# Two transformer blocks on one core: PSUM bank order at the start of two feed-forward layers, and a new placement of output and memory tiles between eight attention heads

## The chip, the cores and the metric

One Trainium2 chip, one core of it. The metric is the device time of one launch in microseconds (us), lower is better. The kernel is written in Python with a tile scheduler: the program states the operations, and the scheduler decides the order on each engine (TensorE = PE, VectorE = DVE, ScalarE = ACT, GpSimd = POOL, SyncE = SP, which here only issues loads).

## The reference

Two blocks over 512 tokens of width 1024, all in fp32. The change touches the two feed-forward layers and the second block's attention:

```python
# first block, after its two attention branches
h = rms_norm(x, pre_ffn_norm)
f = (silu(h @ w_ffn_gate) * (h @ w_ffn_up)) @ w_ffn_down        # 1024 -> 2816 -> 1024
x = x + rms_norm(f, post_ffn_norm)
# second block
fox_o = fox_attention(fq, fk, fv, log_f)                        # 8 heads of 64
z = einsum(q, k) / 8                                            # stick-breaking, 8 heads of 64
log_keep = where(strict, log_sigmoid(-z), 0)
after = reverse_cumsum(log_keep) - log_keep
a = where(strict, exp(log_sigmoid(z) + after), 0)
sb_o = einsum(a, v)
x = x + concat(rmsnorm(fox_o), rmsnorm(sb_o)) @ w_out
x = x + memory_cross_attention(rmsnorm(x), rmsnorm(mem), w_mq, w_mkv, w_mo)   # 256 memory rows
u = conv3(rmsnorm(x) @ w_up)                                    # width 2 * 2816
x = x + (silu(u_gate) * u_val) @ w_down
return rmsnorm(x)
```

## The kernel before, in words

**Matmuls.** Activations lie as 128 x 512 tiles (features on partitions, tokens along the row). Every fp32 operand is split into a high and a low part; `mm3` multiplies a pair by a pair with three matmuls: high by high (L208 in the profile), low by high (L209) and high by low (L210). `wload` loads 128 x 1024 of a weight on SP's queue into one of three buffers (`wr0` to `wr2`); ACT casts the high part (`wh`, L136) and DVE subtracts for the low part (`wl`, L140). A load into a buffer has to wait for the casts out of it. `lin` makes one output tile: a load or two, then 3 matmuls for each 128 rows of the weight, into one PSUM bank.

**Banks.** There are eight PSUM banks of 128 x 512. `share(mm=..., at=..., op=..., st=...)` deals them to four rings by use: `MM()` for linear layers, `AT()` for attention scores, `OP()` for attention outputs, `ST()` for sums of squares. Each call takes the next bank of its ring, so a ring with one bank makes its users wait for one another.

**Norms.** `Stat.done` sums squares with a ones-matmul (L376), takes the inverse root on POOL (`rtok`, L333), turns it with four transposes (L384) into a bank, and copies that bank on ACT to `R` (L390).

**Feed-forward layers.** `first_halves` makes the first six linear tiles in two halves of 256 tokens, so that the first half can begin before the norm of the second is known; it uses banks 0 to 5 for the sums, and 6 and 7 for the sums of squares and `R`. Then come six more `lin`s (L1040 and L1519, from ring 0 to 5 still) and eight tiles of the down projection, each over the six hidden tiles made so far. After that both layers deal all eight banks to `mm`.

**Stick-breaking heads** (L1357 to L1383). The loop runs over nine steps; step `hd` makes the scores and log-keep tiles of head `hd` (`sb_keep`: score matmuls into ring `at`, banks 3 to 6; ACT abs, exp, ln; DVE `e` L1233, `lkh` L1235, `lkl` L1236) and the values of the head before it (`sb_values`: score matmuls again, L1245, L1246, and sums of log-keep L1250, L1251; ACT exp to `aw`, then `ah`; DVE `al`; then `pv2_step`, L1209 and L1210, which add the four query blocks into bank 7, the only bank of ring `op`). At the end of a head `pv2_out` copies half of bank 7 on ACT (`tmp`, L1215) and adds it to the other half on DVE (`so`, L1217). The next head's first L1209 needs bank 7, and so `so`. A short wait of this sort is hidden if other matmuls stand ahead of it.

**Fillers.** For that, `between(fill[hd])` puts tiles of other work behind step `hd`: `y0` to `y7` are output tiles over the forgetting heads (12 matmuls 128x512 each), `k0` to `k7` keys of the memory (24 matmuls 128x256 and one load of 512 KB), `v0` and `v1` values of the memory (48 matmuls 128x512 and four loads of 512 KB). The ninth entry comes after the loop. The scheduler may shift them against the heads, but keeps each engine's work near its place in the program.

**After the loop.** The sums of squares of `so` (L376), tiles of `fill[8]`, four output tiles over `so` (12 matmuls 128x512, `boh`), then the `R` of this norm, then four more output tiles in halves of 256 tokens (`last_halves`) of which the second, in order, takes bank 5 that held the transposes for `R`; then the weights of the cross attention's query (`w_mq`), which ACT casts in the same order in which it copies `R`.

Of the kernel before, what the change touches and what calls it, by code (L numbers as in the profile page):

```python
# [58 lines left out]
def two_blocks(ctx: ExitStack, tc: tile.TileContext, d, dbg=None):  # L59
# [16 lines left out]
    def A(name, dt=F32, cols=T):  # L76
        if cols > 256 or len(spare_half) < 3:
            i = spare.popleft()
            low[0] = min(low[0], len(spare))
            ap = ar.tile([P, T], dt, tag="slot%d" % i, name=name)[:, :cols]  # L80
            owner[id(ap)] = (spare, i, ap, name)
        else:
            i = spare_half.popleft()
            ap = ar.tile([P, 256], dt, tag="half%d" % i, name=name)[:, :cols]
            owner[id(ap)] = (spare_half, i, ap, name)
        return ap

    def free(*xs):
        for x in xs:
            if isinstance(x, (tuple, list)):  # L90
                free(*x)
            else:
                home, i = owner.pop(id(x))[:2]
                home.append(i)
# [13 lines left out]
    def share(**kw):  # L108

        for name, which in kw.items():  # L110
            rings[name] = deque(which)
# [48 lines left out]
    def order(later, earlier):  # L160
        tc.add_manual_dep(later, earlier.name,
                          mybir.DependencyInfo(mybir.DependencyClass.NoSync, mybir.DependencyReason.DATA),
                          reason="table of functions")
# [35 lines left out]
    def wpart(wt, k):  # L199

        step, ws = wt
        hi, lo = ws[k // step][k % step // 4]
        s = slice(k % step % 4 * P, (k % step % 4 + 1) * P)
        return hi[:, s], lo[:, s]

    def mm3(ps, a, b, first, last):
        (ah, al), (bh, bl) = a, b
        r = PE.matmul(ps, lhsT=ah, rhs=bh, start=first, stop=False)  # L208
        PE.matmul(ps, lhsT=ah, rhs=bl, start=False, stop=False)  # L209
        PE.matmul(ps, lhsT=al, rhs=bh, start=False, stop=last)  # L210
        return r.ins
# [35 lines left out]
    def tok_step(ps, h, t, w, first, last):  # L247
        q = slice(t * P, (t + 1) * P)
        return mm3(ps, (h[0][:, q], h[1][:, q]), w, first, last)
# [85 lines left out]
    class Stat:  # L335


        def __init__(self, n, cols=T, esq=None, eadd=None, late=False):
            self.n, self.cols, self.acc, self.late, self.wait = n, cols, {}, late, {}
            self.esq, self.eadd = esq or S, eadd or V  # L340
            self.R, self.r = None, RTOK()
            self.sums, self.turns = {}, {}
# [24 lines left out]
        def done(self, c=None, direct=False):  # L367
# [18 lines left out]
            if direct:  # L386
                return pb[:, :w]
            if self.R is None:
                self.R = A("R")
            S.copy(self.R[:, c], pb[:, :w])  # L390
            return self.R, self.r

# [67 lines left out]
    def evac(ps, name, Rt, scale=None, cols=T):  # L460
        o = A(name)
        if scale is None:
            V.tensor_tensor(o[:, :cols], ps[:, :cols], Rt[:, :cols], ALU.mult)
        else:
            V.scalar_tensor_tensor(o[:, :cols], ps[:, :cols], scale, Rt[:, :cols], ALU.mult, ALU.mult)
        return o
# [29 lines left out]
    def first_halves(at, ns, wts, hs, st, out, before=None, tok=None, tok_out=None):  # L496

        for i, c in enumerate(HALVES):  # L500
            st.done(c)
            ts = range(2 * i, 2 * i + 2) if tok else ()
            tps = [MM() for t in ts]
            pss = [MM() for n in ns]
            last = len(hs) - 1

            def after(r, step):
                for m, earlier in marks:
                    if m == step:
                        order(r, earlier)  # L510

            def tok_k(k, step):
                for t, ps in zip(ts, tps):
                    after(tok_step(ps, hs[k], t, tok[k], k == 0, k == last), step)

            def lin_k(k, j, step):
                hh, hl = hs[k]
                after(mm3(pss[j][:, :256], wpart(wts[j], k), (hh[:, c], hl[:, c]), k == 0, k == last), step)

            if i == 0:  # L520
                marks = [(at[0], st.sums[0]), (at[1], st.turns[0])]
                if before:
                    marks.append((at[2], before.turns[256]))
                for k in range(len(hs)):
                    tok_k(k, k)
                    for j in range(len(ns)):
                        lin_k(k, j, k)
            else:

                marks = [(at[3], st.sums[256]), (at[4], st.turns[256])]  # L530
                for k in range(len(hs)):
                    tok_k(k, k - len(hs))
                for j in range(len(ns)):
                    for k in range(len(hs)):
                        lin_k(k, j, j if k == 0 else None)
            for t, ps in zip(ts, tps):
                tok_out(t, ps)
            for j, n in enumerate(ns):
                out(n, pss[j][:, :256], c)
        free([wt[1] for wt in wts])  # L540
        free(tok or [])
# [80 lines left out]
    st = Stat(DM, esq=S, eadd=V)  # L622
# [16 lines left out]
    free(xs)  # L639
    R, rt = st.done()  # L640
    p0 = evac(pss[0], "p0", R)
# [60 lines left out]
    for t, ps in enumerate(lin_tok(d["w1K"], 0, hs)):  # L702
        x = A("kdx")
# [283 lines left out]
    st = Stat(DM)  # L987
# [28 lines left out]
        V.tensor_tensor(firsts[n][:, c], ps, sth.R[:, c], ALU.mult)  # L1016

    first_halves((6, 7, 3, 2, 4), range(6), ws, hs, sth, first_out, st)
    R = sth.R
    fs = [None] * KD  # L1020
    hid = []
# [5 lines left out]
    st = Stat(DM)  # L1027
# [323 lines left out]
    Rf, _ = stf.done()  # L1351
    close = closing(so, sts, "sb_g")

    fill = [x.split() for x in ('y0 y1 k0 y2|y3 y4|k1 k2|y5 y6 y7 k3|k4 k5||v0 v1||k6 k7').split("|")]

    def between(what, after=None):
        for w in what:  # L1357
# [11 lines left out]
    for hd in range(9):  # L1369
        lks = []  # L1370
        if last:
            op = OP()
# [115 lines left out]

    firsts = {}
    first_halves((2, 3, None, 0, 3), range(6), ws, hs, sth, first_out)  # L1490
    R = sth.R
    hid = []
    st = Stat(DM, late=True)
# [203 lines left out]
```

## Time and profile before

| | |
|---|---|
| median of 3 runs | 1735.14 us (1735.02 to 1739.23) |
| profiled execution | 1737.63 us, its span 1735.8 us, 1.8 us around it |
| PE busy | 1703.2 us (98%), weight loads 1487.2 us (86%) |
| DVE, ACT, POOL busy | 69%, 51%, 5% |
| DMA | 174.30 MB, mean 100 GB/s |
| TensorE's granted clock | full speed in every fortieth of the span |

The span is the time from the first to the last instruction of the profiled execution. In the timeline each row has a start, a duration, engine, line, operation, output and inputs, shape, and in brackets the idle time ahead of it with the instruction that ended it. Matmuls are pipelined: a row's duration is longer than what it adds, so what one matmul costs is read from start to start of two neighbours.

### The profile page before, as it was taken

What the parts mean: (1) busy time and instruction counts of PE and PEld (TensorE: products, weight loads), DVE (VectorE), ACT (ScalarE), POOL (GpSimd) and SP (SyncE); (2) the same over time, 40 slices, a digit from 0 to 9 for tenths busy, and PEclk for the clock granted to TensorE, in tenths of its full rate; (3) what the DMA queues carried; (4) which work ended last, traced back from release to release, by engine and by line L of the source; (5) the groups of instructions that cost most, each with busy time, mean ns of one, the idle gap of its engine ahead of it and who ended that gap; (6) DMA issues with size and microseconds to landing.
All of it is one profiled execution on the core that took longest, in us unless ns stands there. A gap on an engine that the chain in (4) does not pass through costs nothing.

```text
span 1735.8 us, 25856 instructions
## 1 busy us (share of the span) xinstructions
PE 1703.2 (98%) x9706; PEld 1487.2 (86%) x9706; DVE 1197.7 (69%) x2390; ACT 885.5 (51%) x1821; POOL 92.5 (5%) x109
## 2 busy tenths in 40 slices
PE   9999999999999999999999999998999999999998
PEld 7888888888888889989988888887898988988987
DVE  7547764677667757757777666787866598964863
ACT  6534454565444444424445666786525454552653
POOL 1000001000004000000022000000200200000000
PEclk9999999999999999999999999999999999999999
DMA  6212252223640332433324345333314123232321
GB/s 226 85 49 73 66 171 89 75 77 96 200 158 1 107 100 72 125 97 98 123 85 122 96 111 128 103 110 115 117 50 134 50 70 100 92 118 83 103 92 50
DMA packets 63950, 174.30 MB, mean 100 GB/s; under 512 B 8080, under 2 KB 13392, under 8 KB 63824
## 3 DMA queue, kind: packets, MB, share of 16 engines
q1 hardware_dynamic: 63408, 172.44, 32.4%
q8 instruction: 76, 1.25, 0.3%
q14 instruction: 50, 0.41, 0.1%
q10 hardware_dynamic: 288, 0.14, 0.0%
q0 software_dynamic: 128, 0.07, 0.0%
HBM read 153.74 MB, written 4.19 MB: 91 GB/s over the span
## 4 chain that ended last, share of the span: by engine, by line
PE 84%; DVE 7%; ACT 3%; DMA 3%; issue 2%; POOL 1%; POOLq 0%; DVEq 0%; ACTq 0%
PE bank L208 26%; PE bank L210 26%; PE bank L209 26%; DVE wl L140 1%; DMA wr<-w_o_mla 1%; PE bank L1250 1%; DVE hl L142 1%; ACT wh L136 1%; PE bank L828 1%; DVE f L976 1%; DMA wr<-w_mq 1%; DVE sq L362 1%; DMA wr<-w1K 0%; PE bank L1209 0%; PE bank L1210 0%
## 5 line engine op out<-in xcount | busy, mean ns | idle before, releaser
L136 ACT CAST wh<-wr 128x512 fp32r<-128x512 f32 (+2 forms) x534 | 310.7, 605 | 364.4 <-PE bank L209 122.1
L140 DVE TENSOR_TENSOR wl<-wr,wh 128x512 fp32r<-128x512 f32 (+1 forms) x534 | 349.8, 673 | 167.1 <-ACT wh L136 145.8
L208 PE MATMUL bank<-hh,wh 128*128 128x512 f32 (+1 forms) x868 | 306.2, 355 | 1.9 <-DVE z L1016 1.7
L210 PE MATMUL bank<-hh,wl 128*128 128x512 f32 (+1 forms) x868 | 305.9, 354 | 0.8 <-DVE wl L140 0.8
L209 PE MATMUL bank<-hl,wh 128*128 128x512 f32 (+1 forms) x868 | 305.4, 353 | 0.1
L209 PE MATMUL bank<-prl,wh 128*128 128x256 f32 (+1 forms) x760 | 253.5, 334 | 0.0
L210 PE MATMUL bank<-prh,wl 128*128 128x256 f32 (+1 forms) x760 | 253.3, 334 | 0.0
L208 PE MATMUL bank<-prh,wh 128*128 128x256 f32 (+1 forms) x760 | 251.3, 334 | 0.6 <-ACT prh L136 0.6
L210 PEld LDWEIGHTS bank<-hh,wl 128*128 128x128 f32 x868 | 164.7, 190 | 23.2 <-DVE wl L140 2.1
L208 PEld LDWEIGHTS bank<-hh,wh 128*128 128x128 f32 x868 | 164.6, 190 | 23.0 <-ACT hh L138 1.9
L209 PEld LDWEIGHTS bank<-hl,wh 128*128 128x128 f32 x868 | 164.8, 190 | 20.9 <-DVE hl L142 0.6
L208 PEld LDWEIGHTS bank<-prh,wh 128*128 128x128 f32 x760 | 144.3, 190 | 15.0 <-ACT prh L136 1.0
L210 PEld LDWEIGHTS bank<-prh,wl 128*128 128x128 f32 x760 | 144.4, 190 | 14.3 <-DVE wl L140 0.4
L209 PEld LDWEIGHTS bank<-prl,wh 128*128 128x128 f32 x760 | 144.4, 190 | 13.7
L209 PE MATMUL bank<-nl,wh 128*128 128x512 f32 (+1 forms) x440 | 148.4, 337 | 0.0
L208 PE MATMUL bank<-nh,wh 128*128 128x512 f32 (+1 forms) x440 | 148.3, 337 | 0.0
L210 PE MATMUL bank<-nh,wl 128*128 128x512 f32 (+1 forms) x440 | 147.9, 337 | 0.0
L208 PEld LDWEIGHTS bank<-nh,wh 128*128 128x128 f32 x440 | 83.5, 190 | 9.0
L209 PEld LDWEIGHTS bank<-nl,wh 128*128 128x128 f32 x440 | 83.5, 190 | 8.8
L210 PEld LDWEIGHTS bank<-nh,wl 128*128 128x128 f32 x440 | 83.5, 190 | 8.8
L333 POOL TENSOR_TENSOR rtok<-sm,minus_half 128x2 f32<-128x2 f32 (+1 forms) x20 | 17.5, 877 | 1203.0 <-DVE sm L332 1203.0
L136 ACT CAST wh<-s 128x512 fp32r<-128x512 f32 x72 | 43.8, 619 | 69.2 <-DVE s L297 40.4
(400 smaller groups left out, 3357.7 us busy)
## 6 DMA issues: line engine op xcount, KB each, us to landing
wr<-w_up SPq DMA_DIRECT2D x38, 512.0 KB, 3.6
wr<-w_fgu SPq DMA_DIRECT2D x32, 512.0 KB, 4.0
wr<-w1T SPq DMA_DIRECT2D x16, 512.0 KB, 3.5
wr<-w_gate SPq DMA_DIRECT2D x16, 512.0 KB, 4.0
wr<-w_fd SPq DMA_DIRECT2D x16, 512.0 KB, 4.0
wr<-w2T SPq DMA_DIRECT2D x16, 512.0 KB, 3.8
wr<-w_dn SPq DMA_DIRECT2D x16, 512.0 KB, 3.5
wr<-w1K SPq DMA_DIRECT2D x12, 512.0 KB, 4.3
```

What stands on the lines that cost most here:

```text
L136: r = S.copy(hi, src) if eh is S else V.tensor_copy(hi, src)
L140: q = el.tensor_tensor(lo, src, f(hi), ALU.subtract)
L142: q = V.scalar_tensor_tensor(lo, src, scale, f(hi), ALU.mult, ALU.subtract)
L208: r = PE.matmul(ps, lhsT=ah, rhs=bh, start=first, stop=False)
L209: PE.matmul(ps, lhsT=ah, rhs=bl, start=False, stop=False)
L210: PE.matmul(ps, lhsT=al, rhs=bh, start=False, stop=last)
L333: G.tensor_tensor(y, v, minus_half[:, :y.shape[1]], ALU.pow)
L362: i = self.eadd.tensor_tensor(acc, acc, q[:, :w], ALU.add)
L828: PE.transpose(tp[:, i * P:(i + 1) * P], ps_tiles[i][:, b * P:(b + 1) * P], C("ident"))
L976: r = V.scalar_tensor_tensor(fs[k][:, c], fs[k][:, c], vcol(gain, k), st.R[:, c], ALU.mult, ALU.mult)
L1250: PE.matmul(z[:, (b2 - b) * P:w], lhsT=lt, rhs=part[:, :T - b2 * P], start=False, stop=False)
```

## The change

Three edits. Behind `first_halves` of each feed-forward layer the ring of banks is dealt anew: all eight to `mm`, in the order 6, 7, 0 to 5 (before: the six banks 0 to 5 go on). And the list of fillers is another.

```diff
@@ -1016,6 +1016,7 @@
     first_halves((6, 7, 3, 2, 4), range(6), ws, hs, sth, first_out, st)
+    share(mm=(6, 7, 0, 1, 2, 3, 4, 5), at=(), op=(), st=())
     R = sth.R
@@ -1351,7 +1352,7 @@
-    fill = [x.split() for x in ('y0 y1 k0 y2|y3 y4|k1 k2|y5 y6 y7 k3|k4 k5||v0 v1||k6 k7').split("|")]
+    fill = [x.split() for x in ('k0 y0 y1|y2 y3 y4|k1 y5 y6|y7 k2 k3|v0|k4 k5|v1|k6|k7').split("|")]
@@ -1488,6 +1489,7 @@
     first_halves((2, 3, None, 0, 3), range(6), ws, hs, sth, first_out)
+    share(mm=(6, 7, 0, 1, 2, 3, 4, 5), at=(), op=(), st=())
     R = sth.R
```

By step of the loop (0 to 7, then after it) the fillers stand so:

| step | 0 | 1 | 2 | 3 | 4 | 5 | 6 | 7 | after |
|---|---|---|---|---|---|---|---|---|---|
| before | y0 y1 k0 y2 | y3 y4 | k1 k2 | y5 y6 y7 k3 | k4 k5 | none | v0 v1 | none | k6 k7 |
| changed | k0 y0 y1 | y2 y3 y4 | k1 y5 y6 | y7 k2 k3 | v0 | k4 k5 | v1 | k6 | k7 |

Lines behind L1018 are one higher in the changed kernel, behind L1490 two.

What this does to the order is shown at three places. In these rows the number behind a name tells buffers apart, and a bracket names the engine that the row waits for.

**PE at the change from head 6 to head 7**, before: the last matmuls of head 6 into bank 7, then the first of head 7.

```order
L1250 MATMUL bank6_72<-lkl_12242,incl_r_172 128x128
L1251 MATMUL bank6_72<-nstrict_r_178,ident_r_176 128x128
L1209 MATMUL bank7_73<-ah_12252,v2_10506 128x128 [waits Activation_49]
L1210 MATMUL bank7_73<-al_12253,v2_10506 128x128 [waits DVE_49]
L1209 MATMUL bank7_73<-ah_12274,v2_10488 128x512 [waits DVE_49]
L1210 MATMUL bank7_73<-al_12275,v2_10488 128x512
L1209 MATMUL bank7_73<-ah_12291,v2_10494 128x384 [waits Activation_49]
```

And in the changed kernel (L1210 is its first line of a head's output):

```order
L208 MATMUL bank2_68<-boh_12049,wh_12464 128x512
L209 MATMUL bank2_68<-bol_12050,wh_12464 128x512
L210 MATMUL bank2_68<-boh_12049,wl_12465 128x512
L210 MATMUL bank0_66<-boh_11180,wl_12425 128x512 [waits DVE_49]
L208 MATMUL bank0_66<-boh_11617,wh_12424 128x512
L209 MATMUL bank0_66<-bol_11618,wh_12424 128x512
L210 MATMUL bank0_66<-boh_11617,wl_12425 128x512
L208 MATMUL bank0_66<-boh_12049,wh_12424 128x512
L209 MATMUL bank0_66<-bol_12050,wh_12424 128x512
L210 MATMUL bank0_66<-boh_12049,wl_12425 128x512
L1210 MATMUL bank7_73<-ah_12313,v2_10488 128x512 [waits Activation_49]
L1211 MATMUL bank7_73<-al_12314,v2_10488 128x512 [waits DVE_49]
```

Before, nothing stands between the last matmul of head 6 into bank 7 and the first of head 7. In the changed order 18 matmuls 128x512 of output tiles over `so` (10 are shown) stand directly ahead of head 7's first, and ahead of these head 7's score matmuls; these 18 stood further back before.

**PE behind the loop**, where the transposes for `R` stand. Before, they lie among output tiles of the full 512 tokens, and the matmul that needs bank 5 again (`boh_11180` with `wh_12509`) comes 24 rows later:

```order
L208 MATMUL bank1_67<-boh_11617,wh_12444 128x512
L209 MATMUL bank1_67<-bol_11618,wh_12444 128x512
L384 MATMUL bank5_71<-con_160,rtok8_117 128x128 [waits Pool_49]
L384 MATMUL bank5_71<-con_160,rtok8_117 128x128 x3
L210 MATMUL bank1_67<-boh_11617,wl_12445 128x512
L208 MATMUL bank1_67<-boh_11957,wh_12444 128x512
```

In the changed kernel it comes 5 rows later:

```order
L208 MATMUL bank4_70<-boh_12049,wh_12504 128x256
L209 MATMUL bank4_70<-bol_12050,wh_12504 128x256
L384 MATMUL bank5_71<-con_160,rtok8_117 128x128 [waits Pool_49]
L384 MATMUL bank5_71<-con_160,rtok8_117 128x128 x3
L210 MATMUL bank4_70<-boh_12049,wl_12505 128x256
L208 MATMUL bank4_70<-boh_12370,wh_12504 128x256
L209 MATMUL bank4_70<-bol_12371,wh_12504 128x256
L210 MATMUL bank4_70<-boh_12370,wl_12505 128x256
L208 MATMUL bank5_71<-boh_11180,wh_12509 128x256 [waits Activation_49]
```

The transposes moved behind matmuls that followed them before, and the wait for `R` moved close behind them. From the L376 matmuls to that wait there are 18 matmuls 128x512, 12 of 128x256 and the transposes in the changed order. On ACT the copy `R` stands behind eight casts of four `w_mq` loads before and, in the changed kernel, behind six casts of three; of the first `w_mq` load both casts stand between `tmp` of head 7 and the squares of `so` there.

**PE in the second feed-forward layer's down projection**, where the sixth hidden tile (`prh_14666`) is first used. Before:

```order
L209 MATMUL bank4_70<-prl_14583,wh_14783 128x512
L210 MATMUL bank4_70<-prh_14582,wl_14784 128x512
L209 MATMUL bank5_71<-prl_14583,wh_14811 128x512
L210 MATMUL bank5_71<-prh_14582,wl_14812 128x512
L208 MATMUL bank0_66<-prh_14386,wh_14861 128x512 [waits Activation_49]
L209 MATMUL bank0_66<-prl_14387,wh_14861 128x512
L208 MATMUL bank2_68<-prh_14666,wh_14701 128x512 [waits Activation_49]
```

In the changed kernel:

```order
L210 MATMUL bank2_68<-prh_14498,wl_14944 128x512
L208 MATMUL bank2_68<-prh_14582,wh_14947 128x512
L209 MATMUL bank2_68<-prl_14583,wh_14947 128x512
L210 MATMUL bank2_68<-prh_14582,wl_14948 128x512
L208 MATMUL bank0_66<-prh_14386,wh_14861 128x512 [waits Activation_49]
L209 MATMUL bank0_66<-prl_14387,wh_14861 128x512
L208 MATMUL bank4_70<-prh_14666,wh_14701 128x512 [waits Activation_49]
```

With two more banks one more output tile (bank 2, `wh_14943`) can begin before the sixth hidden tile is there: 15 of its matmuls 128x512 now stand ahead of the waiting row. In the first feed-forward layer the order of PE is the same as before but for the numbers of the banks.

## Rows read from the trace of the kernel before

**Rows 1.** The page: its span, the busy time of each engine, and the granted clock of TensorE in 40 equal slices (9 is 90% or more of full speed).

```profile
span 1735.8 us, 25856 instructions
PE 1703.2 (98%) x9706; PEld 1487.2 (86%) x9706; DVE 1197.7 (69%) x2390; ACT 885.5 (51%) x1821; POOL 92.5 (5%) x109
PEclk9999999999999999999999999999999999999999
```

**Rows 2.** The waits of PE within the loop over the stick-breaking heads (1086 to 1213.4 us): what waited for what, us in total, times, longest.

```profile
PE bank L1209 <- DVE so L1217: 4.6, 3, 2.4
PE bank L1245 <- ACT aw L171: 1.4, 3, 0.6
PE bank L1245 <- DVE e L1233: 1.1, 1, 1.1
PE bank L210 <- DVE wl L140: 0.8, 2, 0.4
```

**Rows 3.** The timeline of PE, six of the matmuls that waited there: start, duration, and in brackets the wait.

```profile
1113.14 0.50 PE L1245 MATMUL bank<-dbl,stk 128*128 128x512 f32 x1 [0.63 <-ACT aw L171]
...
1159.52 0.50 PE L1209 MATMUL bank<-ah,v 128*128 128x512 f32 x1 [1.44 <-DVE so L1217]
...
1163.69 0.33 PE L1245 MATMUL bank<-dbl,stk 128*128 128x128 f32 x1 [0.62 <-ACT aw L171]
...
1172.90 0.51 PE L1209 MATMUL bank<-ah,v 128*128 128x512 f32 x1 [0.68 <-DVE so L1217]
...
1203.13 0.50 PE L1245 MATMUL bank<-dbl,stk 128*128 128x512 f32 x1 [1.06 <-DVE e L1233]
...
1209.91 0.50 PE L1209 MATMUL bank<-ah,v 128*128 128x512 f32 x1 [2.45 <-DVE so L1217]
```

**Rows 4.** Busy time by stretch, each from the first L1209 of one head to that of the next (heads 2 to 3, 3 to 4, 4 to 5, 5 to 6, 6 to 7): length, then busy us and instructions of PE, PEld, DVE, ACT, POOL, the granted clock, the DMA engines' share and GB/s.

```profile
1131.04:1148.43 17.39, 16.99 (x118) 15.67 (x117) 15.75 (x35) 14.04 (x33) 0.00 (x0) 1.00 0.67 182
1148.43:1159.52 11.09, 9.65 (x71) 9.17 (x69) 8.48 (x21) 8.01 (x20) 0.00 (x0) 1.00 0.16 49
1159.52:1172.90 13.38, 12.02 (x72) 10.49 (x73) 11.60 (x26) 12.79 (x32) 0.00 (x0) 1.00 0.13 39
1172.90:1198.24 25.34, 25.16 (x119) 20.84 (x119) 18.13 (x35) 17.65 (x37) 0.00 (x0) 1.00 0.44 136
1198.24:1209.91 11.67, 8.16 (x59) 7.51 (x57) 8.16 (x18) 9.10 (x25) 0.00 (x0) 1.00 0.21 69
```

**Rows 5.** The timeline of DVE, ACT and PE at the change from head 6 to head 7: the last log-keep tile of head 7, head 6's last matmul into bank 7, and the two steps of its output.

```profile
1205.24 0.29 DVE L1236 SCALAR_TENSOR_TENSOR lkl<-e,lkh 128x128 fp32r<-128x128 f32 x1
...
1207.19 0.28 PE L1210 MATMUL bank<-al,v 128*128 128x128 f32 x1
...
1208.56 0.58 ACT L1215 COPY tmp<-bank 64x512 f32<-64x512 f32 x1
...
1209.18 0.68 DVE L1217 TENSOR_TENSOR so<-bank,tmp 64x512 f32<-64x512 f32 x1
```

**Rows 6.** The timeline of PE: neighbours of 128x512 and of 128x256, for the step from start to start.

```profile
1220.71 0.40 PE L208 MATMUL bank<-boh,wh 128*128 128x512 f32 x1
1220.94 0.39 PE L209 MATMUL bank<-bol,wh 128*128 128x512 f32 x1
...
1229.48 0.28 PE L209 MATMUL bank<-bol,wh 128*128 128x256 f32 x1
1229.60 0.28 PE L210 MATMUL bank<-boh,wl 128*128 128x256 f32 x1
```

**Rows 7.** The timeline of PE behind the loop: the sums of squares, the transposes, and the matmul that takes bank 5 again.

```profile
1219.12 0.95 PE L376 MATMUL bank<-con,sq 128*128 128x2 f32 x8
...
1226.40 0.60 PE L384 MATMUL bank<-con,rtok 128*128 128x128 f32 x4
...
1232.12 0.39 PE L208 MATMUL bank<-boh,wh 128*128 128x256 f32 x1 [1.17 <-ACT R L390]
```

**Rows 8.** The timeline of ACT behind the loop: the squares of the last `so`, three of the four pairs of `w_mq` casts, and the copy of `R`.

```profile
1217.25 0.63 ACT L349 ACTIVATE sq<-so 128x512 f32<-128x512 f32 x1 [0.99 <-DVE so L1217]
...
1224.62 1.15 ACT L136 CAST wh<-wr 128x512 fp32r<-128x512 f32 x2 [1.50 <-DMA wr<-w_mq]
...
1227.64 1.14 ACT L136 CAST wh<-wr 128x512 fp32r<-128x512 f32 x2 [1.88 <-DMA wr<-w_mq]
...
1230.32 1.14 ACT L136 CAST wh<-wr 128x512 fp32r<-128x512 f32 x2 [0.20 <-DMA wr<-w_mq]
1231.48 0.59 ACT L390 COPY R<-bank 128x512 f32<-128x512 f32 x1
```

**Rows 9.** DMA issues of `w_mq`: count, KB each, and the median us from issue to landing; of those issued from 1215 to 1216 us, of those from 1220 to 1222.6 us, and of all.

```profile
wr<-w_mq SPq DMA_DIRECT2D x1, 512.0 KB, 3.7
...
wr<-w_mq SPq DMA_DIRECT2D x3, 512.0 KB, 6.2
...
wr<-w_mq SPq DMA_DIRECT2D x8, 512.0 KB, 4.0
```

**Rows 10.** The timeline of PE: the longest wait in the first feed-forward layer, and the one in the second.

```profile
560.30 0.36 PE L208 MATMUL bank<-hh,wh 128*128 128x256 f32 x1 [1.72 <-DVE z L1016]
...
1448.18 0.50 PE L208 MATMUL bank<-prh,wh 128*128 128x512 f32 x1 [0.62 <-ACT prh L136]
```

## The prediction on record

> **What bounds the kernel now.** I read the page first. PE is busy 1703.2 of 1735.8 us, the next engine, DVE, 69%, and TensorE has its higher clock level, 2.4 GHz, in all 40 slices (granted share 0.9 or more) [rows 1]. So the kernel is a chain of matmuls, and since the change adds and removes no matmul, no cast and no load, it can win only what PE waits: 1735.8 - 1703.2 = 32.6 us over the whole span. The next view is PE's waits within the loop over the stick-breaking heads. They come to 4.6 + 1.4 + 1.1 + 0.8 = 7.9 us, and over half of it is a head's first output matmul waiting for bank 7, that is for the output `so` of the head before [rows 2]. The timeline says where: 1.44, 0.62 and 0.68 us from 1159 to 1173, 1.06 and 2.45 us from 1203 to 1210 [rows 3]. The busy time by stretch says why. From head 5 to head 6 both memory-value tiles stand, and PE is idle 25.34 - 25.16 = 0.18 us; from head 2 to 3 it is idle 0.40 us. From 3 to 4 it is 11.09 - 9.65 = 1.44, from 4 to 5 1.36, from 6 to 7 11.67 - 8.16 = 3.51 us [rows 4]. The last three are the starved stretches: 6.3 us together. The chain that PE waits for there is fixed: head 6's last matmul into bank 7 starts at 1207.19, `tmp` follows at 1208.56, `so` ends at 1209.18 + 0.68 = 1209.86 [rows 5], and head 7 starts at 1209.91 [rows 3]. To hide it, some 2.5 us of other matmuls have to stand in between.
>
> **The change, part by part.** PE's unit prices are steps from start to start: 128x512 takes 1220.94 - 1220.71 = 0.23 us, 128x256 0.12 us [rows 6].
>
> *Fillers, what they hide.* From head 6 to 7 nothing stood between; the changed order puts 18 matmuls 128x512 directly ahead of head 7's first, 18 x 0.23 = 4.1 us, and head 7's score matmuls too, more than the 2.5 us wanted. The memory-value tiles (48 x 0.23 = 11.0 us each) no longer stand together in a stretch that idled 0.18 us anyway: one goes to the stretch of 1.44 us. The key tiles (24 x 0.12 = 2.9 us each) stand in steps 5 and 7, one of which was empty. All three starved stretches so get more than their wait. I take the whole 6.3 us as removed: **-6.3**. The bounds are 0 (the waits only move) and -7.9 (all of the loop's waits go).
>
> *Fillers, what is late next.* Every moved tile brings its loads on SP, its casts on ACT and its subtractions on DVE. The stretch from head 4 to 5 already has ACT busy 12.79 of 13.38 us [rows 4]: there ACT, not PE, sets the pace, and two more casts of `wh` at 0.57 each (1.15 for two) [rows 8] fall into heads that had none. I take 0.8 us for that. On DVE `lkl` of head 7 (0.29) now stands behind `so` (0.68) and so behind `tmp` (0.58) [rows 5]; PE's sums of log-keep wait for it: half of 1.55, 0.7 us. And the 18 matmuls ahead of head 7 need three `w_out` tiles cast in time, where before they came later: 0.8 us, the cast and subtraction of one tile less what its two buffers of lead give. Together **+2.3**, bounds 0 and 4.9 (twice the largest wait that stands there now, 2.45 [rows 3]). The loads themselves cost nothing: the stretch with eight value loads moved 136 GB/s and the one with `y` tiles 182 GB/s, both with PE idle under 0.5 us [rows 4], and the changed list spreads them. Without that cover a load costs what one of `w_mq` takes, about 4 us [rows 9].
>
> *Behind the loop.* What is used to hide head 7 is missing later. The sums of squares end at 1219.12 + 0.95 = 1220.07; the matmul that takes bank 5 again could have started at 1232.12 - 1.17 = 1230.95 [rows 7]. So before 10.9 us of matmuls stand from the sums to this wait. Now there are 18 x 0.23 + 12 x 0.12 + the transposes, 0.45 = 6.0 us. The copy of `R` ends at 1231.48 + 0.59 = 1232.07, 12.0 us after the sums, and it is late because it stands on ACT behind `w_mq` casts that wait for loads (1.50, 1.88, 0.20 us) [rows 8]. If it stays at 12.0, PE waits 6.0 instead of 1.2 us; if it only needs its transposes, it ends some 6.1 us after the sums and PE waits 0.1. So the term is between +4.9 and -1.1. In the changed order three pairs of casts stand ahead of it, not four, which takes off 1.3 us (a pair and its wait: 1.14 + 0.20) and leaves 10.7. Of the waits for loads, 1.50 + 1.88 + 0.20 = 3.6 us, I take off half, 1.8, since the order lets the first of these loads out before the sums and not behind them. That makes 8.9 us, about the middle of 12.0 and 6.1: a wait of 2.9 us in place of 1.2, **+1.7**.
>
> *Second feed-forward layer.* PE waits 0.62 us there for the sixth hidden tile [rows 10]. The changed order puts 15 matmuls of another output tile, 15 x 0.23 = 3.4 us, ahead of it: **-0.6**. If the two banks were not free, the wait would be as before, 0.
>
> *First feed-forward layer.* Its order is the same, and its one long wait, 1.72 us [rows 10], lies within `first_halves`, ahead of the new line. **0**; the two banks go to tiles that wait for nothing now.
>
> The sum: -6.3 + 2.3 + 1.7 - 0.6 = -2.9 us. The profiled execution took 1737.63 us (span 1735.8 and 1.8 around it), 2.5 us above the median of the runs, 1735.14. The terms are differences, so I set them against both: 1734.7 for an execution like the profiled one, **1732.2 us** as the median.
>
> **The rivals.** I call a difference under 0.3% (5.2 us: 1729.9 to 1740.3) no change, as it is about what a measurement of this kernel can tell.
>
> *Loads come sooner, and the gain stays.* The last `w_mq` loads before took 6.2 us each, three at once, while one alone took 3.7 [rows 9]. If the spread list leaves them alone, they land 2.5 us sooner: `R` ends some 6.9 us after the sums, PE waits 0.9 us (-0.3 against before instead of +1.7), and the 0.8 us for `w_out` go: -6.3 + 1.5 - 0.3 - 0.6 = -5.7, 1729.4 us. For it: fewer loads stand right behind the loop. Against it: the three go out within 2.4 us in either order. The Trainium skill, "DMA: Bandwidth & Descriptors", section "Anatomy of one DMA", fits a DMA (on GpSimd's path, these are on SP's) with about 2.0 us plus its bytes over 436 GB/s, which for 512 KB gives an estimate of 3.2 us whatever else is in flight. By that rule this rival is the forecast; the rows, 6.2 us for three at once, disagree.
>
> *The waits only move.* ACT's 96% in the stretch from head 4 to 5 becomes the pace of more stretches, with as much idle as before, and the tail loses what the order adds: -6.3 + 4.9 + 1.7 - 0.6 = -0.3, 1734.8 us. For it: ACT is busy 12.79 us where PE is 12.02 [rows 4]. Against it: where the value tiles stand, PE has 25.16 us for ACT's 17.65, and the changed list uses that surplus twice.
>
> *Slower: `R` behind the casts.* The squares of `so`, on ACT, now stand behind the first `w_mq` pair; if this load takes 6.2 us and not 3.7, the sums come 2.5 us late with little left to hide it, and `R` still comes 12.0 us after them, behind three more pairs. That is +2.5 + 4.9. With 4.9 of new waits in the loop it would be -6.3 + 4.9 + 2.5 + 4.9 - 0.6 = +5.4, 1740.5 us. `R` decides: the change loses there from the point where it ends more than 6.0 + 1.2 = 7.2 us after the sums, and the whole is slower than before once the loop and layers keep less than that loss. For it: the order of ACT's queue is fixed, and its row shows a wait for `w_mq` ahead of every pair [rows 8]. Against it: it takes the late end of three terms at once.
>
> **How the numbers follow.** The forecast, 0.52: its own range is 1729.5 to 1735. Loads sooner, 0.26: 1727.5 to 1731. Waits only move, 0.15: 1733 to 1737. Slower, 0.07: 1737 to 1742. Faster by over 0.3% takes most of the second case, 0.22 of 0.26, and the low end of the first, 0.08: 0.30. Slower is the last case, 0.07, and no change the rest, 0.63. The range from 1727.5 to 1737.0 leaves out the last case and the tails of the others, under 2 in 10.
>
> **What would show it.** In the changed kernel's profile: no wait of head 7's first output matmul (L1210 there) for `so`, and starved stretches with under 1 us idle; `lkl` or `wl` as the new releasers within the loop, 1 to 4 us in all; behind the loop, the wait of the matmul into bank 5 for ACT's `R` at 2 to 4 us, where it was 1.17, with `w_mq` loads as what ACT waits for ahead of it; no wait for `prh` in the second layer's down projection; nothing new in the first. I am wrong if `so` still ends waits of over 2 us, if the wait for `R` is under 1 or over 5 us, if the head stretches idle as much as before, or if waits arise in a feed-forward layer that had none.

## The result, and the profile after

The changed kernel takes **1726.23 us** (median of 6 runs, 1724.92 to 1726.83), the kernel before 1736.05 us (6 runs): a ratio of 0.9941 with a 95% interval of 0.9930 to 0.9951. It is faster by 9.8 us, outside the forecast range and more than three times the forecast gain of 2.9 us. The profiled execution took 1726.83 us. Its page, to be held against [rows 1]:

```profile
span 1725.1 us, 25847 instructions
PE 1700.7 (99%) x9706; PEld 1485.8 (86%) x9706; DVE 1197.4 (69%) x2390; ACT 886.9 (51%) x1821; POOL 92.0 (5%) x109
PEclk9999999999999999999999999999999999999999
```

PE's idle time fell from 32.6 to 1725.1 - 1700.7 = 24.4 us, 8.2 us less. Its busy time fell too, by 2.5 us, with the same 9706 matmuls. Of these, 1.4 us lie in the places named below, where something of a wait is counted as busy; the rest lies ahead of the heads, 0.7 us of it in the first 28 us.

**Where the time came from.** Both traces have the same number of matmuls in each stage, so the n-th matmul of one (counted by start, from 0) can be laid beside the n-th of the other wherever the order agrees again:

| matmul, place | start before | start after | difference | won in this stretch |
|---|---|---|---|---|
| 5830, ahead of the heads | 1070.74 | 1069.72 | -1.02 | 1.0 |
| 6805, output tiles behind the heads | 1240.84 | 1232.84 | -8.00 | 7.0 |
| 6949, cross attention's first halves | 1260.46 | 1250.94 | -9.52 | 1.5 |
| 8100, second feed-forward layer | 1438.34 | 1428.77 | -9.57 | 0.05 |
| 8254, behind its first down projection | 1470.99 | 1460.26 | -10.73 | 1.2 |
| 9705, the last | 1729.10 | 1718.36 | -10.74 | 0.0 |

Of the first 1.0 us, 0.5 is there by matmul 100 (28 us) and 0.9 by matmul 500 (115 us), ahead of everything that the change touches. The executions of the other runs start matmul 5830 between 2.1 us earlier and 1.5 us later than that of the kernel before, so this is a difference between two executions. The other 9.7 us lie in three places: the heads, the cross attention's first halves and the second feed-forward layer.

**The heads.** PE's waits in the loop (1083 to 1213 us) answer to [rows 2]:

```profile
PE bank L208 <- ACT wh L136: 0.7, 1, 0.7
PE bank L1246 <- ACT aw L171: 0.5, 1, 0.5
PE bank L1211 <- DVE al L140: 0.2, 1, 0.2
```

No wait for `so` is left; 4.6 us in three waits stood there. By stretch from head to head (2 to 3, and so on to 6 to 7; columns as in [rows 4]):

```profile
1125.31:1144.30 18.99, 18.77 (x127) 17.29 (x127) 15.91 (x35) 16.01 (x38) 0.00 (x0) 1.00 0.62 168
1144.30:1163.86 19.56, 19.56 (x117) 17.49 (x117) 13.65 (x27) 13.55 (x31) 0.00 (x0) 1.00 0.42 133
1163.86:1180.13 16.27, 15.74 (x99) 13.72 (x98) 14.21 (x32) 14.49 (x38) 0.00 (x0) 1.00 0.22 66
1180.13:1196.12 15.99, 15.99 (x97) 14.35 (x96) 11.65 (x24) 11.90 (x25) 0.00 (x0) 1.00 0.33 99
1196.12:1208.84 12.72, 12.17 (x68) 9.90 (x67) 9.81 (x23) 9.94 (x26) 0.00 (x0) 1.00 0.24 82
```

Length less PE's busy time gives 0.22, 0, 0.53, 0 and 0.55 us, 1.3 together; in [rows 4] it was 0.40, 1.44, 1.36, 0.18 and 3.51, 6.9. The lengths themselves are now even, 13 to 20 us instead of 11 to 25. At the change from head 6 to 7 PE, ACT and DVE show why:

```profile
1201.52 0.33 PE L1211 MATMUL bank<-al,v 128*128 128x128 f32 x1
...
1201.88 0.58 ACT L1216 COPY tmp<-bank 64x512 f32<-64x512 f32 x1 [0.98 <-PE bank L1211]
...
1202.50 0.68 DVE L1218 TENSOR_TENSOR so<-bank,tmp 64x512 f32<-64x512 f32 x1
...
1208.62 0.39 PE L210 MATMUL bank<-boh,wl 128*128 128x512 f32 x1
1208.84 0.39 PE L1210 MATMUL bank<-ah,v 128*128 128x512 f32 x1
```

`so` is there at 1203.18, and head 7's first matmul comes 5.7 us later, right behind the `boh` matmuls and without a wait. The chain is covered, and it is shorter as well: `tmp` and `so` take the same 0.58 and 0.68 us as in [rows 5], but `tmp` starts 0.36 us behind the start of head 6's last matmul instead of 1.37. Before, `aw` and `ah` of head 7 stood ahead of `tmp` on ACT, the last of them this cast:

```profile
1207.89 0.64 ACT L136 CAST ah<-aw 128x512 fp32r<-128x512 f32 x1
```

From head 6's last matmul to the end of `so` it is 1.7 us now and was 2.7; 5.7 us of other matmuls hide either.

**Behind the loop.** These rows answer to [rows 7], [rows 8] and [rows 9]:

```profile
1216.13 0.95 PE L376 MATMUL bank<-con,sq 128*128 128x2 f32 x8
...
1222.10 0.60 PE L384 MATMUL bank<-con,rtok 128*128 128x128 f32 x4
...
1224.35 0.39 PE L208 MATMUL bank<-boh,wh 128*128 128x256 f32 x1 [1.19 <-ACT R L390]
```
```profile
1212.98 1.14 ACT L136 CAST wh<-wr 128x512 fp32r<-128x512 f32 x2 [1.69 <-DMA wr<-w_mq]
1214.03 0.62 ACT L349 ACTIVATE sq<-so 128x512 f32<-128x512 f32 x1
...
1218.40 1.14 ACT L136 CAST wh<-wr 128x512 fp32r<-128x512 f32 x2 [1.80 <-DMA wr<-w_mq]
1221.32 2.37 ACT L136 CAST wh<-wr 128x512 fp32r<-128x512 f32 x4 [1.77 <-DMA wr<-w_mq]
1223.71 0.59 ACT L390 COPY R<-bank 128x512 f32<-128x512 f32 x1
```
```profile
wr<-w_mq SPq DMA_DIRECT2D x3, 512.0 KB, 4.1
```

(the last row: the median of the three issued from 1214.5 to 1218 us). The wait for `R` is what it was, 1.19 against 1.17 us. The matmuls that cover it shrank as forecast, to 1223.16 - 1217.08 = 6.1 us from the sums to the wait, but `R` ends 1224.30 - 1217.08 = 7.2 us after the sums instead of 12.0. Of these 4.8 us, 1.3 are the pair of casts that no longer stands ahead. The rest is the third of the three loads. It goes out at 1217.76, 0.7 us after the sums, where it went out at 1222.37, 2.3 us after them; and it lands 1.7 us faster, as its own row shows, first the changed kernel's, then that of the kernel before:

```profile
wr<-w_mq SPq DMA_DIRECT2D x1, 512.0 KB, 4.8
...
wr<-w_mq SPq DMA_DIRECT2D x1, 512.0 KB, 6.5
```

**The cross attention's first halves.** Of the kernel before, three rows that stood in no group (the sums, `rtok` on POOL, the transposes), and of the changed kernel the same three:

```profile
1250.80 0.50 PE L376 MATMUL bank<-con,sq 128*128 128x2 f32 x4
...
1255.36 0.71 POOL L333 TENSOR_TENSOR rtok<-sm,minus_half 128x2 f32<-128x2 f32 x1 [1.22 <-DVE sm L332]
...
1256.12 0.43 PE L384 MATMUL bank<-con,rtok 128*128 128x128 f32 x2 [1.25 <-POOL rtok L333]
```
```profile
1246.45 0.50 PE L376 MATMUL bank<-con,sq 128*128 128x2 f32 x4
...
1248.39 0.71 POOL L333 TENSOR_TENSOR rtok<-sm,minus_half 128x2 f32<-128x2 f32 x1 [0.83 <-DVE sm L332]
...
1250.49 0.38 PE L384 MATMUL bank<-con,rtok 128*128 128x128 f32 x2
```

The sums and the transposes stand about 30 matmuls 128x256 (3.6 us) further back in the changed order, behind the same work of ACT, DVE and POOL; `rtok` is ready 2.7 us after the sums begin, where it took 5.3, and so 1.4 us ahead of the transposes. Nothing in the fillers' list names this stage, but the list moved it: with the fillers alone the transposes stand at the same new place (the 6945th matmul, before the 6913th), and with both last key tiles behind the loop at the old one (the 6912th). Why the scheduler does so was not looked into.

**What a wait costs.** PE around the wait of the second feed-forward layer, before the change:

```profile
1447.18 0.39 PE L209 MATMUL bank<-prl,wh 128*128 128x512 f32 x1
1448.18 1.19 PE L208 MATMUL bank<-prh,wh 128*128 128x512 f32 x4 [0.62 <-ACT prh L136]
1449.34 0.50 PE L210 MATMUL bank<-prh,wl 128*128 128x512 f32 x1
1449.34 0.19 PEld L210 LDWEIGHTS bank<-prh,wl 128*128 128x128 f32 x1 [0.40 <-DVE wl L140]
1449.67 0.40 PE L208 MATMUL bank<-prh,wh 128*128 128x512 f32 x1
```

From 1447.18 to 1448.18 it is 1.00 us where a step is 0.23: the wait costs 0.77, not the 0.62 in brackets. The step behind it is slow too: the row's second matmul starts at 1448.52, 0.34 us after the first. Two steps then take 0.23, and the one to 1449.34 takes 0.36: the weight load there waits for `wl`, a second, shorter wait that no bracket of PE shows. The step behind that one takes 1449.67 - 1449.34 = 0.33. In all 1.1 us, some 0.9 for the first wait and 0.2 for the second. In the changed kernel both are gone, and with them the 1.2 us of the table. The Trainium skill, "TensorE: Matmul & The Clock Gate", section "Single matmul latency", gives a matmul on its own, with bf16 operands, a fixed time of about 0.17 us beside that of its columns. The 0.77 - 0.62 = 0.15 us here agrees with it: by about so much the row ahead of the wait, 0.39 us long, outlasts its step of 0.23. The slower step after a wait is this trace's own.

### The profile page after: what moved, and what is told of

It is laid out like the page before. It is cut to its first block, busy times and chain, and to the rows that moved or that the text cites. A ratio compares the mean times of both kernels' runs of the same rounds, so it can differ in the third digit from the quotient of the medians.

```text
span 1725.1 us, 25847 instructions
## 1 busy us (share of the span) xinstructions
PE 1700.7 (99%) x9706; PEld 1485.8 (86%) x9706; DVE 1197.4 (69%) x2390; ACT 886.9 (51%) x1821; POOL 92.0 (5%) x109
## 3 DMA queue, kind: packets, MB, share of 16 engines
q8 instruction: 76, 1.25, 0.3%
## 4 chain that ended last, share of the span: by engine, by line
PE 88%; DVE 4%; DMA 3%; ACT 2%; issue 1%; POOL 0%; POOLq 0%; DVEq 0%; SPq 0%; ACTq 0%
PE bank L208 27%; PE bank L210 27%; PE bank L209 27%; DVE wl L140 1%; PE bank L828 1%; PE bank L1251 1%; ACT wh L136 1%; DVE f L976 1%; DMA wr<-w_mq 0%; DMA wr<-w1K 0%; PE bank L1211 0%; DVE hl L142 0%; PE bank L1210 0%; DMA wr<-w1T 0%; PE bank L376 0%
```

## The experiments

Theory A: the gain is made of PE's waits, place by place: those of the head loop, that for `rtok`, that for `prh`, each with a restart behind it. Theory B: the banks carry it, by stalls that no row shows. Each run was timed with the kernel before on the same chip; the changed kernel was not timed again, so what a run loses against it is the difference of two medians, or of two ratios to the kernel before.

**The fillers alone.** Edit against the kernel before:

```diff
-    fill = [... 'y0 y1 k0 y2|y3 y4|k1 k2|y5 y6 y7 k3|k4 k5||v0 v1||k6 k7' ...]
+    fill = [... 'k0 y0 y1|y2 y3 y4|k1 y5 y6|y7 k2 k3|v0|k4 k5|v1|k6|k7' ...]
```

> Only the new list of fillers, both feed-forward layers as before. Theory A (the gain is the waits of the head loop and what the order behind it moves): the loop's waits for the output of the head before go, about -7 us with the restart of PE behind each wait; the wait of the transposes for rtok in the cross attention's first halves (1.25 us) goes, -1.5; the wait of 0.62 us in the second layer's down projection stays. Together some -8.6 us against the kernel before, about 1727.4. Theory B (the banks carry the gain, by stalls that no wait row shows): -4 us or less, 1732 or more.

Measured: 1727.48 us, before 1736.3; ratio 0.9945 (0.9933 to 0.9958). That is 8.8 us, where theory A had 8.6. In the loop no wait for `so` is left and three short ones of 1.3 us stay, the wait for `rtok` is gone, and the one for `prh` still stands at 0.6 us.

**The bank rings alone.** One added line each, in the second layer and in the first:

```diff
     first_halves((2, 3, None, 0, 3), range(6), ws, hs, sth, first_out)
+    share(mm=(6, 7, 0, 1, 2, 3, 4, 5), at=(), op=(), st=())
```

> Only the eight-bank ring in the second feed-forward layer. Theory A: the wait of 0.62 us for prh in the down projection goes together with the slow restart behind it, -1.1 us, about 1734.9; heads and tail as before. Theory B: -3 us or more, 1733 or less.

> Only the eight-bank ring in the first feed-forward layer. Theory A: the order of PE is the same but for bank numbers and no wait stood behind first_halves: 0 us, about 1736.0. Theory B: -2 to -3 us, about 1733.5.

Measured: 1734.65 us, ratio 0.9992 (0.9983 to 1.0001), and 1736.04 us, ratio 0.9997 (0.9988 to 1.0006). Neither interval excludes 1, so the times alone show only that neither ring carries the gain. The trace of the second layer shows the size: no wait for `prh` is left, and matmul 8254 starts 1.16 us earlier, against matmul 8100, than before. Theory B falls.

**Both last key tiles behind the loop.** Edit against the changed kernel: `v1|k6|k7` becomes `v1||k6 k7`.

> The changed kernel with both last memory-key tiles behind the loop, so that step 7 has no filler. In the order, 1.8 us of matmuls then stand between head 6's last and head 7's first output matmul (6.7 us in the changed kernel, 0 before), and the transposes for the cross attention's norm stand where they stood before the change. Theory A: the wait for the output of head 6 is back with 0.8 to 1.0 us (1.2 with the restart), the wait for rtok is back with 1.2 us (1.5): +2.7 against the changed kernel, about 1729. Theory B (where the tile stands does not matter): 1726.2.

Measured: 1734.48 us, ratio 0.9989 (0.9980 to 0.9997): 8 us of the 9.8 are lost, three times what was expected. PE's waits from 1190 to 1213 us:

```profile
PE bank L1210 <- ACT ah L136: 2.3, 2, 1.6
PE bank L1246 <- DVE e L1234: 1.9, 1, 1.9
PE bank L1211 <- DVE al L140: 0.4, 2, 0.2
```

The wait for `so` that theory A had is not there. Not `so` is late but the whole head: score, exp, log, split, one after the other on ACT and DVE, with little for PE beside it. The wait for `rtok` is back with 0.7 us, not 1.2. And behind such pauses PE itself is slower. In these stretches (columns as in [rows 4]) PE first rests, then works at half the clock:

```profile
1196.00:1199.00 3.00, 0.88 (x3) 0.37 (x2) 1.96 (x4) 3.00 (x8) 0.00 (x0) 1.00 0.24 84
1199.00:1206.00 7.00, 6.91 (x25) 5.89 (x25) 5.18 (x15) 2.90 (x9) 0.00 (x0) 0.53 0.24 76
1206.00:1210.00 4.00, 2.12 (x15) 1.68 (x14) 2.06 (x4) 3.37 (x10) 0.00 (x0) 0.93 0.19 64
1210.00:1213.00 3.00, 3.00 (x9) 2.71 (x10) 2.74 (x6) 1.73 (x4) 0.00 (x0) 0.50 0.20 58
```

PE is busy for 0.88 of 3 us up to 1199, and then has a granted share of 0.53 for 7 us: 1.2 instead of 2.4 GHz. A step of 128x512 takes 0.43 us there:

```profile
1199.77 0.63 PE L1251 MATMUL bank<-lkh,incl_r 128*128 128x512 f32 x1
1200.19 0.63 PE L1251 MATMUL bank<-lkl,incl_r 128*128 128x512 f32 x1
```

From matmul 5830 to 6805 this execution takes 8.4 us longer than that of the changed kernel: PE idles 3.6 us more, and the same matmuls take 4.8 us more, which is mostly the price of the lower clock. All 11 executions show a mean granted clock of 0.993 to 0.996, the changed kernel's six 0.998 or 0.999. So the place of one 2.9 us tile is worth 8 us, about half of it by the clock.

**Both value tiles in one step.** Against the changed kernel: `v0|k4 k5|v1` becomes `|k4 k5|v0 v1`.

> The changed kernel with both memory-value tiles in step 6 again (step 4 without a filler); k6 and k7 as in the changed kernel. In the order, 2.2 us of matmuls stand from head 3's last to head 4's first output matmul and 0.3 us from head 6's to head 7's (7.4 and 6.7 in the changed kernel); the transposes of the cross attention's norm stand as late as in the changed kernel. Theory A (PE waits what the matmuls in between leave of about 2.6 us): waits for so of 0.4 and 2.3 us and their restarts, +3 us against the changed kernel, about 1729. Theory C (as in the run with both key tiles behind the loop: where a head has too little else, its own chain over ACT and DVE is bare too and TensorE's granted clock falls behind the pauses): +7 to +9, 1733 to 1735, with the granted clock under 1 in the stretch behind head 6. Theory B (the place of the value tiles does not matter): 1726.2.

Measured: 1732.19 us, ratio 0.9971 (0.9959 to 0.9982), 5 to 6 us over the changed kernel, between A's 3 and C's 7 to 9. Of A's two waits for `so` one is there, 0.3 us at the change to head 4; head 7 waits for `ah` instead (1.69 us), and the granted clock is 0.66 from 1210 to 1215 us. What neither had: the wait for `R` grows to 2.5 us, and one of 1.2 us for a cast `wh` of a value tile arises at 1170. The second suggests that the even spread also keeps the loads and casts of the tiles apart; neither was followed further.

**The second half of the list alone.** Against the kernel before: steps 0 to 3 as before, then `v0|k4 k5|v1|k6|k7`.

> The kernel before with the second half of the new list alone: steps 0 to 3 as before, then v0, k4 k5, v1, k6 and k7 behind the loop; feed-forward layers as before. In the order at least 2.8 us of matmuls stand at every change of heads. Theory A: the waits for so go as in the changed kernel; of the changes in steps 0 to 3 only the wait of 0.7 us for the last forgetting head stays; about -7.5 us against the kernel before, 1728.7. Theory B (spreading the output tiles in steps 0 to 3 carries half of the gain): -4, 1732.

Measured: 1733.34 us, ratio 0.9980 (0.9971 to 0.9989): 3.4 us faster than the kernel before (1736.71 on this chip). Theory A's 7.5 missed; theory B's 4 is near. No wait for `so` is left, as A said, but others came:

```profile
1142.51 0.73 PE L208 MATMUL bank<-wh,mh 128*128 128x512 f32 x2 [1.52 <-ACT wh L136]
...
1203.18 0.33 PE L1226 MATMUL bank<-dbl,stk 128*128 128x128 f32 x1 [1.13 <-DVE e L1233]
...
1237.21 0.39 PE L208 MATMUL bank<-boh,wh 128*128 128x256 f32 x1 [1.71 <-DVE y L1402]
```

With `y5 y6 y7 k3` still in step 3 and `v0` right behind, a cast `wh` for a value tile is late (the first of these rows); covering the heads is not enough, the weights of the cover have to be there. Both halves of the list are needed.

**The transposes later.** Against the kernel before, in the cross attention's first halves only (`done` is split into `sum_up` and `turn`):

```diff
-            st.done(c)
+            split = late is not None and i == 0
+            (st.sum_up if split else st.done)(c)
...
                     for j in range(len(ns)):
                         lin_k(k, j, k)
+                    if split and k == late:
+                        st.turn(c)
...
-    first_halves((5, 7, None, 2, 3), range(6), ws, hs, sth, first_q)
+    first_halves((5, 7, None, 2, 3), range(6), ws, hs, sth, first_q, late=5)
```

> The kernel before, with one edit: in the cross attention's first halves the four transposes for R of the first 256 tokens are put out later, behind 21 more matmuls 128x256 (2.4 us); fillers and banks as before. Theory A (the wait of 1.25 us for rtok is a matter of where the transposes stand, and goes with 2.4 us more in front): -1.5 us against the kernel before, about 1734.7. Rival (the products of the first half then wait for R instead): 0, 1736.2.

Measured: 1734.79 us, ratio 0.9987 (0.9978 to 0.9996), and no wait for `rtok` from 1235 to 1260 us. From matmul 6805 to 6949 this execution is 1.5 us shorter than that of the kernel before. The 1.5 us that the changed kernel won there are a matter of where the transposes stand, and can be had without the fillers.

**The copy of R.** Three tries against the changed kernel, to take away its last wait of over 1 us in this region. On DVE (`V.tensor_copy` instead of `S.copy` for this norm):

> The changed kernel, with the copy of R for the norm over the stick-breaking heads on DVE instead of ACT; nothing else moves on PE. Theory A (R is late because it stands on ACT behind w_mq casts that wait for their loads): PE's wait of 1.19 us for the bank falls to 0 to 0.2, -1.2 to -1.4 us, about 1724.9. Rival (R is bound by its own transposes, or DVE's queue is as late): the wait stays at 1 us or more, 1726.2.

Measured: 1728.1 us (1726.13 to 1730.14), ratio to the kernel before 0.9948 (0.9936 to 0.9961). The rival is right: PE waits 2.19 us for `R` instead of 1.19. By the time alone the run can't be told from the changed kernel, whose interval is 0.9930 to 0.9951. The copy stands behind the four subtractions `wl` of the same loads:

```profile
1223.83 2.51 DVE L140 TENSOR_TENSOR wl<-wr,wh 128x512 fp32r<-128x512 f32 x4 [1.69 <-ACT wh L136]
1226.26 0.69 DVE L390 COPY R<-bank 128x512 f32<-128x512 f32 x1
```

Ahead of the second and third pair of casts, or of all (`hold[0] = sts.copied` before those `wtile` calls, which orders the casts behind the copy):

> The changed kernel, with the copy of R put ahead of the second and third pair of w_mq casts on ACT; nothing moves on PE. Theory A (R waits on ACT behind casts that wait for loads): R follows its transposes by 0.8 us instead of 1.6, PE's wait of 1.19 us falls to 0.3, -0.9 to -1.0 us, about 1725.2. Rival (the casts, now later, hold the cross attention's first matmuls): a wait for wh there takes its place, 1726.2 or more.

> As the run with R ahead of the second and third pair, but ahead of all w_mq casts, so that the squares of so are not behind the first pair either. Theory A: sums 1 us earlier against the matmuls, R ready when PE asks, the wait of 1.19 us gone: -1.2 to -1.4, about 1724.9. Rival: the last w_mq weights come late for the first halves, with a wait for wh or wl of 1 us or more there: 1726 or more.

Measured: 1730.01 us, ratio 0.9966 (0.9952 to 0.9980), and 1730.49 us, ratio 0.9968 (0.9957 to 0.9979). The mechanism of theory A is there and its gain is not. In the first of the two, the wait for `R` falls to 0.2 us, but two others arise behind it:

```profile
1225.60 0.39 PE L208 MATMUL bank<-boh,wh 128*128 128x256 f32 x1 [0.20 <-ACT R L390]
...
1235.61 0.39 PE L208 MATMUL bank<-boh,wh 128*128 128x256 f32 x1 [2.30 <-DVE y L1403]
...
1246.79 0.39 PE L208 MATMUL bank<-hh,wh 128*128 128x256 f32 x1 [1.65 <-DVE y L1403]
```

The casts, and with them DVE's `wl`, now fall between the products `y` that free the banks: five `wl` from 1228.0 to 1235.2 us, where the changed kernel has three from 1226.8 to 1231.7. In the second the waits are for `wh` (2.0 us) and `y` (2.0 us), and the granted clock of its profiled execution fell to about half from 1202 to 1209 and from 1236 to 1240 us, so that its trace does not tell what the waits alone cost.

Banks 6 and 7 for the output tiles behind the heads:

```diff
-    share(mm=(0, 1, 2, 3, 4, 5), at=(6, 7), op=(), st=(6, 7))
+    share(mm=(6, 7, 4, 5, 0, 1, 2, 3), at=(), op=(), st=())
     last_halves(range(4, 8), wl4, so, so_out)
+    share(mm=(0, 1, 2, 3, 4, 5), at=(6, 7), op=(), st=(6, 7))
```

> The changed kernel, and behind the heads the output tiles over so in halves open their ring with banks 6 and 7, which nothing uses there: 24 matmuls 128x256 (2.8 us) that stood behind the wait for R stand ahead of the sums or of the wait. Theory A (the time of R is set by the w_mq loads on ACT's queue, so matmuls that can be done without R cover it): the wait of 1.19 us for R goes to 0, -1.2 to -1.4 us, about 1724.9. Rival (R comes as much later, being behind one more pair of casts and behind later sums): the wait stays, 1726.2 or more.

Measured: 1734.43 us, ratio 0.9988 (0.9979 to 0.9997). The rival is right and too mild: the wait for `R` is 2.5 us, that for `rtok` is back with 2.6, one for `y` has 1.7. Up to matmul 6805 this execution is not slower than that of the changed kernel; all of the loss lies in the cross attention's first halves, where the transposes stand at the 6909th matmul again, 36 rows ahead of their place in the changed kernel. No run beat the changed kernel.

## Why the prediction was wrong

The mechanism was right in the main: starved heads get cover, `so` is no longer waited for, the wait for `prh` goes, the first layer gives nothing. Direction too. What failed are three terms of the sum, and one that it lacks, all to the same side.

1. **"I take the whole 6.3 us as removed", and the "+2.3".** I counted three starved stretches. The even spread took the loop's other waits as well: PE's idle time there fell from 8.2 to 2.2 us, short pauses included, where my terms leave 7.9 - 6.3 + 2.3 = 3.9. One more wait of 0.7 us went, for the last forgetting head's output, which lay ahead of the window that I had read. And the slower steps behind the waits, which I did not count, went with them, 0.5 us. So the stretch from matmul 5830 to 6805 won 7.0 us, where my three terms for it, -6.3 + 2.3 + 1.7, made -2.3. That the new waits come to 2.2 us, close to my 2.3, is luck: I named `lkl` and `wl`, and what stands there is `wh` (0.7), `aw` (0.5), `al` (0.2) and shorter pauses. I also took the chain behind `so` as fixed, and it is 1.0 us shorter now; and of steps 5 and 7, which got key tiles, both were empty before, not one.
2. **"+1.7" for `R`.** It was 0.0. The pair of casts less was worth 1.3, as I had it. For the loads I took off 1.8 by halving ACT's waits (the 0.20 of the last is taken off twice); they gave 3.4, by so much sooner after the sums the third pair of casts ends. About half of that is that its load goes out sooner, half that it lands faster. So `R` ends 7.2 us after the sums, not 8.9. The rival "Loads come sooner" is closer with its 6.9, for which it shows no working. Its price of a load was also nearer: a median of 4.1 us for three, between its 3.7 and the 6.2 before, which is a median too, of 4.3, 6.2 and 6.5. That rival, 1729.4, came nearest and missed as well, since it shares the other terms. The estimate of 3.2 us from the Trainium skill, "DMA: Bandwidth & Descriptors", section "Anatomy of one DMA — SWDGE (gpsimd) path", is still short of the 4.1. That the loads were faster because fewer stood in their way was not tested by itself.
3. **The wait for `rtok`, -1.5, is in no term.** The order showed it: transposes 32 rows further back. I had followed the order up to the wait for `R` and not through the next stage, and left the 1.25 us wait out of the rows. The run with late transposes shows that this is all of it.
4. **"-0.6" for the second layer.** It was -1.2, since behind the bracket of 0.62 came slower steps and a second wait, for `wl`.

With these the sum is -7.0 - 1.5 - 1.2 = -9.7, against 9.8 measured; that they agree to 0.1 us is more than runs of the kernel before, 1735.02 to 1739.23 us, can vouch for. What I gave as a reason for caution, "ACT, not PE, sets the pace" from head 4 to 5, did not hold: ACT is busy 14.49 of 16.27 us there now, and PE 15.74. The wait of 0.52 us for `aw` in this stretch is all that is left of it.

## What to carry to other kernels

When fillers are moved, read the new order to the end of the stage behind them and beyond, since the edit can move waits that it never names. Price a wait on TensorE by the starts of the matmuls around it, not by the bracket, and a head without any filler by its whole chain, not by the one wait that ends last. A wait such as that for `R` here need not be won by moving the copy that ends it: none of the three runs that did so gained time.

## What the runs showed of the hardware

A pause of PE can cost twice: by the wait, and by a granted clock that falls behind it. In the run with both key tiles behind the loop the granted clock fell to 0.5 for some 7 and 3 us behind pauses of 1.9 and 1.6 us. One and the same wait does it in one execution and not in another: behind that of 2.45 us at 1209.91 [rows 3] the granted clock stayed at 1.00 in the profiled execution of the kernel before, and in that of the run with the second layer's ring alone, with the same wait, it was this:

```profile
1209.60:1213.00 3.40, 3.38 (x10) 2.95 (x11) 2.86 (x6) 1.83 (x4) 0.00 (x0) 0.53 0.23 78
```

There 1.6 us were lost by 1213 us, and 1.3 of them won back by 1234 at the wait for `R`, of which nothing is left in this execution: here a delay ahead of a wait that other engines set cost little.

The Trainium skill, "TensorE: Matmul & The Clock Gate", section "HAM oscillation — how this bites in real kernels", tells of waits for DMA that bring the clock down again and again. In the first of these runs waits for ACT and DVE did so, twice.

The fall is not bound to a long wait either. In the run with `R` ahead of all casts, PE has the changed kernel's order in the loop, is busy for 5.45 us from 1196 to 1202 as there, and has no wait over 0.15 us from 1112 to 1234 us. Yet in its profiled execution the clock fell:

```profile
1196.00:1202.00 6.00, 5.45 (x28) 3.96 (x27) 5.81 (x15) 4.69 (x14) 0.00 (x0) 1.00 0.18 46
1202.20:1209.10 6.90, 6.90 (x28) 6.32 (x27) 4.05 (x8) 5.12 (x12) 0.00 (x0) 0.51 0.32 109
```

The changed kernel has 1.00 from 1202.2 to 1209.1 us, and 42 matmuls to these 28. Of the six profiled executions with this order of the loop, one shows such a fall there; of the four with the order of the kernel before, two. So the cover does not rule it out.
